# A two-layer decoder trunk on one core: the first loads in the order of use, on two queues, with the start of the schedule rearranged

## The chip, the core and the metric

The kernel runs on one core of a Trainium2 chip. A core has five engines that take instructions in order and wait for each other by semaphores: TensorE (PE) multiplies and transposes, ScalarE (ACT) and VectorE (DVE) work elementwise, GpSimd (POOL) sets up constants and issues some transfers, SyncE (SP) issues most transfers. Transfers between memory and the core's buffers are carried out by 16 DMA engines. The metric is the device time of one execution in microseconds (us), as the median of several; lower is better. The kernel before takes 962.69 us (three runs, 961.73 to 963.36).

## The reference, cut to what matters

Layer 0 is a forgetting attention, layer 1 a dilated window attention. Each is followed by an embedding term; 512 tokens, model width 1024, everything in float32.

```python
h = x
# layer 0
h = h + fox_mixer(rms_norm(h, fox_norm[0]), fox_w_in[0], fox_b_f[0], fox_w_out[0])
h = h + (p[0] @ ple_w_up[0]) * sigmoid(h @ ple_w_gate[0])
# layer 1
h = h + dilated_mixer(rms_norm(h, dil_norm[0]), dil_w_in[0], dil_w_out[0])
h = h + (p[1] @ ple_w_up[1]) * sigmoid(h @ ple_w_gate[1])
return rms_norm(h, final_norm)

# fox_mixer begins with
proj = rms_norm(h) @ w_in          # q, k, v, z (1024 columns each) and f (16 columns)
c = cumsum(log_sigmoid(f + b_f))   # the forget gates
# logit[t, s] = q_t . k_s / 8 + c[t] - c[s], causal softmax, values, silu(z), @ w_out
```

The work at the start needs x, p[0], the norm's gain, ple_w_up[0] and fox_w_in.

## The kernel before, in words

**Products in three parts.** A float32 operand is kept as two parts: `hi`, its copy rounded to the type that PE multiplies in one go (ACT, line 86 for weights and 436 for activations), and `lo`, the rest (DVE, lines 87 and 437). A product is hi·hi + hi·lo + lo·hi, so three matmuls (lines 298, 299, 300).

**Weights** come through the class `Stream` as granules in a fixed list: first two halves of `ple_w_up[0]` (256 rows by 512 columns each), then four granules of `fox_w_in` for the first half of v (I call them F0 to F3, 512 KB each), the 16 columns of f, four more granules for v, and so on. There are four buffers for raw granules and five for split ones. `prefetch(n)` issues the loads up to granule n on SP's queue; a granule's buffer is free for its next load when both parts of the split are made.

**The start**, which the change touches, has these steps.
1. POOL makes the identity matrix `ident` (lines 443, 444).
2. SP issues the loads. p[0] comes in two halves of its 256 columns (`load_p0`, line 527), each followed by one half of granule 0 (line 71); then block 0 of x (line 536), granule 1 (line 73), block 1, the gain (line 465), blocks 2 and 3, F0 to F2.
3. `p_columns` transposes p (PE, line 507), two groups of four, and splits it to `pT`; after each group one half of granule 0 is split (`then(k)`, line 509).
4. `up_rows` computes p @ ple_w_up (48 matmuls, in two column halves of four token blocks). ACT evacuates each block (line 517) to a tile `upo`, of which there are three, and SP stores it to a scratch tensor `up_dram` at once (line 518). It is read back only at the end of layer 0.
5. `start_block(b)` normalises a block of 128 tokens: two square sums on ACT (line 487), nine small DVE instructions for 1/sqrt (`rstd_of`, lines 476 to 481), the product `xn` on DVE (line 552). `side` then pushes eight transposes (PE, line 456) and the split into `xnT`. Blocks 0 and 1 are started inside `up_rows`, blocks 2 and 3 inside step 6.
6. `token_rows` computes the first half of v (I call it V0): 96 matmuls, 24 per token block, over F0 to F3.
7. Then `f_rows`: 16 matmuls for the forget gates, whose first is line 625. `f_evac` computes the gates on ACT and DVE; POOL sends the result `cc` to where the scores read it.

The order in which instructions stand on each engine is made by a scheduler from the dependencies and the order in which the code issues them. `tc.issue_after(i)` keeps what stands under it behind instruction `i` in that order. Layer 0's heads, the middle part and layer 1 follow; the change doesn't touch their code.

## Time and profile before

| What | Value |
|---|---|
| Median of three runs | 962.69 us |
| The profiled execution's own time | 960.73 us |
| Its span, first to last instruction | 958.9 us |
| PE busy | 935.7 us, 98% of the span |
| DVE busy | 702.0 us, 73% |
| ACT busy | 503.3 us, 52% |
| Identity matrix finished by POOL | 1.37 us |
| PE's products start 0.43 us apart until, 0.23 from | 12.54 us |
| Last stores of line 518 in layer 0 issued | 27.21 us |
| cc sent by POOL (line 646) | 66.40 us |
| First score product on PE (line 682) | 89.25 us |

The profile is of one execution. Times in the rows further down are counted from its first instruction. A busy share is an average over stages: what the start costs is read from the first 50 us, in which each engine's instructions can be followed one by one. The time between two starts on PE is the pace of its products; the duration of one is longer, since they overlap.

### The profile page before, as it was taken

The numbers are of one execution on the slowest core, as the hardware profiler recorded it, in microseconds if no ns is written. First come the engines' busy times: TensorE is split into PE (matmuls) and PEld (weight loads), VectorE is DVE, ScalarE is ACT, GpSimd is POOL, SyncE is SP. The second block draws the span as 40 slices with busy tenths as digits, with TensorE's granted clock in tenths as the row PEclk, the third lists the DMA queues.
The fourth block names the chain that finished last, engine by engine and source line by source line (L and its number), as shares of the span: only waits on it lengthen the run. The fifth ranks groups of instructions, "written<-read, shape, count | busy, mean of one in ns | idle before, by whom it ended". The sixth has DMA issues, their size and how long they took to land.

```text
span 958.9 us, 15802 instructions
## 1 busy us (share of the span) xinstructions
PE 935.7 (98%) x6000; PEld 841.2 (88%) x6000; DVE 702.0 (73%) x1421; ACT 503.3 (52%) x926; POOL 56.7 (6%) x119
## 2 busy tenths in 40 slices
PE   6999999999999999999999999999999999999996
PEld 5888888888888887899999999999999999987885
DVE  5765877777764478887897887758788797675446
ACT  7455766766752248543565554443446455564233
POOL 0000000000027000100000000010000000010000
PEclk9999999999999999999999999999999999999999
DMA  8453222221146227353323223335332322256102
GB/s 295 146 154 88 67 67 67 67 66 67 67 154 217 90 88 241 113 152 88 111 70 108 69 66 111 111 107 135 96 103 74 104 79 68 99 163 232 68 0 89
DMA packets 126588, 104.58 MB, mean 109 GB/s; under 512 B 14736, under 2 KB 105872, under 8 KB 126512
## 3 DMA queue, kind: packets, MB, share of 16 engines
q1 hardware_dynamic: 121728, 90.59, 31.0%
q0 software_dynamic: 4608, 12.72, 4.1%
q8 instruction: 47, 0.77, 0.3%
q14 instruction: 29, 0.24, 0.1%
q10 hardware_dynamic: 176, 0.26, 0.1%
HBM read 92.93 MB, written 10.55 MB: 108 GB/s over the span
## 4 chain that ended last, share of the span: by engine, by line
PE 82%; DVE 7%; DMA 5%; ACT 4%; issue 2%; SPq 1%; DVEq 0%; POOLq 0%; ACTq 0%
PE ps L347 8%; PE ps L349 8%; PE ps L348 8%; PE ps L300 8%; PE ps L298 8%; PE ps L299 8%; PE ps L328 4%; PE ps L330 4%; PE ps L329 4%; PE ps L404 3%; PE ps L406 3%; PE ps L407 3%; PE ps L715 2%; PE ps L1024 2%; DMA oth<-stb 2%
## 5 line engine op out<-in xcount | busy, mean ns | idle before, releaser
L87 DVE TENSOR_TENSOR wlo<-wraw,whi 128x1024 fp32r<-128x1024 f32 (+1 forms) x78 | 94.4, 1211 | 102.8 <-ACT whi L86 102.2
L347 PE MATMUL ps<-comb,whi 128*128 128x256 f32 x448 | 131.0, 292 | 0.0
L86 ACT ACTIVATE whi<-wraw 128x1024 fp32r<-128x1024 f32 (+1 forms) x78 | 81.7, 1048 | 92.7 <-PE ps L300 60.2
L349 PE MATMUL ps<-comb,wlo 128*128 128x256 f32 x448 | 127.0, 284 | 0.0
L348 PE MATMUL ps<-comb,whi 128*128 128x256 f32 x448 | 126.7, 283 | 0.0
L347 PE MATMUL ps<-xn2T,whi 128*128 128x256 f32 x336 | 97.1, 289 | 0.0
L108 ACT ACTIVATE whi<-ws 128x1024 fp32r<-128x1024 f32 x56 | 59.2, 1057 | 68.7 <-PE ps L348 64.9
L349 PE MATMUL ps<-xn2T,wlo 128*128 128x256 f32 x336 | 95.1, 283 | 0.0
L348 PE MATMUL ps<-xn2T,whi 128*128 128x256 f32 x336 | 95.0, 283 | 0.0
L348 PEld LDWEIGHTS ps<-comb,whi 128*128 128x128 f32 x448 | 85.8, 192 | 0.4
L347 PEld LDWEIGHTS ps<-comb,whi 128*128 128x128 f32 x448 | 85.8, 192 | 0.4
L349 PEld LDWEIGHTS ps<-comb,wlo 128*128 128x128 f32 x448 | 85.8, 192 | 0.0
L109 DVE TENSOR_TENSOR wlo<-ws,whi 128x1024 fp32r<-128x1024 f32 x56 | 68.3, 1219 | 14.7 <-ACT whi L108 14.7
L328 PE MATMUL ps<-xnT,whi 128*128 128x512 f32 x192 | 78.5, 409 | 0.0
L330 PE MATMUL ps<-xnT,wlo 128*128 128x512 f32 x192 | 75.4, 393 | 0.0
L329 PE MATMUL ps<-xnT,whi 128*128 128x512 f32 x192 | 75.0, 391 | 0.0
L108 ACT ACTIVATE whi<-wraw 128x1024 fp32r<-128x1024 f32 (+1 forms) x56 | 47.3, 844 | 36.7 <-PE ps L348 20.9
L348 PEld LDWEIGHTS ps<-xn2T,whi 128*128 128x128 f32 x336 | 64.4, 192 | 0.0
L347 PEld LDWEIGHTS ps<-xn2T,whi 128*128 128x128 f32 x336 | 64.4, 192 | 0.0
L349 PEld LDWEIGHTS ps<-xn2T,wlo 128*128 128x128 f32 x336 | 64.3, 191 | 0.0
L109 DVE TENSOR_TENSOR wlo<-wraw,whi 128x1024 fp32r<-128x1024 f32 (+1 forms) x56 | 53.0, 950 | 2.1 <-ACT whi L108 2.0
L298 PE MATMUL ps<-whi,hT 128*128 128x512 f32 (+1 forms) x136 | 51.7, 380 | 0.0
(245 smaller groups left out, 2466.1 us busy)
## 6 DMA issues: line engine op xcount, KB each, us to landing
wraw<-in_dil_w_in_dram SPq DMA_DIRECT2D x80, 512.0 KB, 3.8
wraw<-in_fox_w_in_dram SPq DMA_DIRECT2D x32, 512.0 KB, 4.2
wraw<-in_ple_w_gate_dram SPq DMA_DIRECT2D x16, 512.0 KB, 3.7
up_dram<-upo SPq DMA_DIRECT2D x16, 256.0 KB, 4.1
wraw<-in_fox_w_out_dram SPq DMA_DIRECT2D x8, 512.0 KB, 3.4
up<-up_dram POOLq DMA_DIRECT2D x8, 512.0 KB, 5.7
wraw<-in_dil_w_out_dram SPq DMA_DIRECT2D x8, 512.0 KB, 3.4
x_in<-in_x_dram SPq DMA_DIRECT2D x4, 512.0 KB, 9.0
```

The lines of the kernel that those rows point to most:

```text
L86: ACT.activation(hi[:, k], t[:, k], AF.Copy)
L87: DVE.tensor_tensor(lo[:, k], t[:, k], f32(hi)[:, k], OP.subtract)
L108: ACT.activation(hi[:, :n], src, AF.Copy)
L109: DVE.tensor_tensor(lo[:, :n], src, f32(hi[:, :n]), OP.subtract)
L298: PE.matmul(o, xh, wh[:, kk, c0:c1], start=first, stop=False)
L299: PE.matmul(o, xh, wl[:, kk, c0:c1], start=False, stop=False)
L328: PE.matmul(t, wh[:, k, :], xh, start=(k == 0), stop=False)
L329: PE.matmul(t, wh[:, k, :], xl, start=False, stop=False)
L330: PE.matmul(t, wl[:, k, :], xh, start=False, stop=(k == KT - 1))
L347: PE.matmul(o, ah, bh, start=(first and k == 0), stop=False, skip_group_check=not first)
L348: PE.matmul(o, ah, bl, start=False, stop=False, skip_group_check=not first)
L349: PE.matmul(o, al, bh, start=False, stop=(last and k == 3), skip_group_check=not first)
```

## The change

Six edits, all in the start, and one in the gate evaluation.

1. p[0] is one load (`load_p`, line 501 of the new file: 4 KB that lie together per partition) on SP's queue. The first half of granule 0 goes out on ACT's queue at the same time, the second on SP's. After them come block 0 of x, granule 1, the gain, F0, block 1, F1, block 2, F2, block 3, F3.
2. Fourteen transposes of `ident` into an unused bank stand ahead on PE (line 540), with no reader.
3. Granule 0's first half is split after p's first transposes are issued and before pT's first split; the second half's split is kept behind that of pT on ACT.
4. One table load, of the set that has both logarithm and exponential, stands at the start. The load of the other set, which the scheduler had put at the very start, is kept behind `cc`; the two loads inside `f_evac` fall away.
5. Blocks 0 and 1 of x are started at steps 3 and 7 of `up_rows`, blocks 2 and 3 at steps 3 and 6 of V0 (before: 4 and 7, 1 and 4); `side.flush()` after `up_rows` falls away; `xn` has one buffer, not two.
6. The eight stores of `up_rows` are kept in a list and issued in V0's steps 8 to 15, behind the load of F3; `upo` has eight buffers, not three.

The core of the diff:

```diff
             if i == 0:
                 for k in range(nk):
-                    self.before[k]()
-                    SP.dma_start(t[:, k, :], src[:, k, :])
+                    (ACT, SP)[k].dma_start(t[:, k, :], src[:, k, :])
             else:
-                SP.dma_start(t[:, :, :cw], src)
+                load = SP.dma_start(t[:, :, :cw], src)
+                if i == g_v[0][3]:
+                    last["load"] = load
...
+            if k == 0:
+                then(0)
             split_out(pT[0][:, k, :], pT[1][:, k, :], t)
-            then(k)
+            if k == 0:
+                with tc.issue_after(last["act"].ins):
+                    then(1)
...
-                u = pool.tile([P, 512], F32, tag="upo", bufs=3, name=nm("upo"))
+                u = pool.tile([P, 512], F32, tag="upo", bufs=(8, 3)[L], name=nm("upo"))
                 ACT.activation(u, t, AF.Copy, scale=0.5)
-                SP.dma_start(up_dram[L][b][:, c * 512:(c + 1) * 512], u)
+                store = lambda c=c: SP.dma_start(up_dram[L][b][:, c * 512:(c + 1) * 512], u)
+                if L == 0:
+                    stores.append(store)
+                else:
+                    store()
...
-        pin = sp.tile([P, NB, 256], F32, tag="pin", bufs=1, name=nm("pin"))
-
-        def load_p0(k):
-            SP.dma_start(pin[:, :, k * P:(k + 1) * P],
-                         p[0, 0, :, k * P:(k + 1) * P].rearrange("(p b) c -> p b c", p=P))
-
-        ws.before = [lambda: load_p0(0), lambda: load_p0(1)]
+        pin = load_p(0, sp)
         ws.prefetch(1)
+        ACT.preload_act_table_set("natural_log_exp_and_others")
+        idle = bank(7)
+        for n in range(14):
+            PE.transpose(idle[:, n % 4 * P:(n % 4 + 1) * P], ident, ident)
...
         load_x(0)
         ws.prefetch(2)
+        gain = load_gain(fox_norm, sp, "gain")
+        ws.prefetch(3)
         load_x(1)
-        gain = load_gain(fox_norm, sp, "gain")
+        ws.prefetch(5)
         load_x(2)
         load_x(3)
-        ACT.preload_act_table_set("natural_log_exp_and_others")
...
-            xn = sp.tile([P, D], F32, tag="xn", bufs=2, name=nm("xn"))
+            xn = sp.tile([P, D], F32, tag="xn", bufs=1, name=nm("xn"))
...
                 side.tick()
-                if n in (4, 7):
-                    start_block((n - 4) // 3)
-            side.flush()
+                if n in (3, 7):
+                    start_block((n - 3) // 4)
         for n, _ in enumerate(token_rows(xnT, g_v[0], blk, v_evac(0), group=4)):
             side.tick()
-            if n in (1, 4):
-                start_block(2 + (n - 1) // 3)
+            if n in (3, 6):
+                start_block(1 + n // 3)
+            if n > 7:
+                with tc.issue_after(last["load"].ins):
+                    stores.pop(0)()
...
-        ACT.activation(cc[:16], u, AF.Copy)
+        done = ACT.activation(cc[:16], u, AF.Copy)
         DVE.tensor_tensor(cc[64:80], u, f32(cc[:16]), OP.subtract)
-        ACT.preload_act_table_set("exp_and_others")
+        with tc.issue_after(done.ins):
+            ACT.preload_act_table_set("exp_and_others")
```

How the order of instructions moves, at three places. The new file's lines are two or more higher than the old one's for the same code.

SP's queue, its first loads, before (`pin` is p, `wraw` a raw granule, of w_up or w_in, `x_in` a block of x):

```order
L527 DMA pin_88<-in_p_dram 128x4x128
L71 DMA wraw_89<-in_ple_w_up_dram 128x512
L527 DMA pin_88<-in_p_dram 128x4x128
L71 DMA wraw_89<-in_ple_w_up_dram 128x512
L536 DMA x_in<-in_x_dram 128x1024
L73 DMA wraw_96<-in_ple_w_up_dram 128x2x512
L536 DMA x_in<-in_x_dram 128x1024
L465 DMA gain_99<-in_fox_norm_dram 128x1024
L536 DMA x_in<-in_x_dram 128x1024 x2
L73 DMA wraw_132<-in_fox_w_in_dram 128x2x512
```

The same of the changed kernel; the other half of granule 0 stands on ACT:

```order
L501 DMA pin_88<-in_p_dram 128x1024
L70 DMA wraw_90<-in_ple_w_up_dram 128x512
L545 DMA x_in<-in_x_dram 128x1024
L72 DMA wraw_111<-in_ple_w_up_dram 128x2x512
L467 DMA gain_113<-in_fox_norm_dram 128x1024
L72 DMA wraw_115<-in_fox_w_in_dram 128x2x512
L545 DMA x_in<-in_x_dram 128x1024
L72 DMA wraw_118<-in_fox_w_in_dram 128x2x512
L545 DMA x_in<-in_x_dram 128x1024
L72 DMA wraw_120<-in_fox_w_in_dram 128x2x512
```

F0 (`wraw_132`, now `wraw_115`) moves from the eleventh load to the seventh, counting ACT's, and ahead of blocks 1 to 3 of x.

DVE, from the sixth small step of block 0's 1/sqrt to its `xn` and the first step of block 1, before:

```order
L480 SCALAR_TENSOR_TENSOR rstd_198<-rstd_198 128x1
L481 SCALAR_TENSOR_TENSOR rstd_198<-rstd_198 128x1
L480 SCALAR_TENSOR_TENSOR rstd_198<-rstd_198 128x1
L481 SCALAR_TENSOR_TENSOR rstd_198<-rstd_198 128x1
L552 SCALAR_TENSOR_TENSOR xn_208<-x_in,rstd_198,gain_99 128x1024
L476 TENSOR_SCALAR rstd_259<-ss_254 128x1
```

The same of the changed kernel:

```order
L482 SCALAR_TENSOR_TENSOR rstd_192<-rstd_192 128x1
L88 TENSOR_TENSOR wlo_206<-wraw_115,whi_205 128x1024
L483 SCALAR_TENSOR_TENSOR rstd_192<-rstd_192 128x1
L482 SCALAR_TENSOR_TENSOR rstd_192<-rstd_192 128x1
L483 SCALAR_TENSOR_TENSOR rstd_192<-rstd_192 128x1
L562 SCALAR_TENSOR_TENSOR xn_202<-x_in,rstd_192,gain_113 128x1024
L478 TENSOR_SCALAR rstd_265<-ss_260 128x1
```

The low part of F0's split now stands behind the sixth of the nine steps; before, it stood behind `xn` of block 1.

ACT, from the split of granule 1 on, before (`junk` is a square sum of a block of x, `upo` an evacuation of p @ w_up):

```order
L86 ACTIVATE whi_128<-wraw_96 128x1024
L487 ACTIVATE junk_194,ss_193<-x_in 128x512
L517 ACTIVATE upo_144<-ps_127 128x512
L487 ACTIVATE junk_196,ss_193<-x_in 128x512
L487 ACTIVATE junk_255,ss_254<-x_in 128x512
L517 ACTIVATE upo_154<-ps_147 128x512
```

The same of the changed kernel:

```order
L87 ACTIVATE whi_148<-wraw_111 128x1024
L489 ACTIVATE junk_188,ss_187<-x_in 128x512
L523 ACTIVATE upo_158<-ps_147 128x512
L523 ACTIVATE upo_167<-ps_160 128x512
L489 ACTIVATE junk_190,ss_187<-x_in 128x512
L87 ACTIVATE whi_205<-wraw_115 128x1024
```

Two evacuations stand between the two square sums of block 0, and the high part of F0's split follows them, ahead of block 1's square sums. On PE (not shown) 14 transposes of `ident` stand first, the first two token blocks of `up_rows` take turns, and before V0 there are eight transposes of block 0 alone, where there were those of blocks 0 and 1; block 1's stand inside V0's first token block, behind 21 matmuls.

## Rows read from the trace of the kernel before

**Rows 1.** Timeline, PE, start: start us, us, engine, line, operation, out<-in, [idle before]

```profile
4.04 1.09 PE L507 MATMUL ps<-ident,pin 128*128 128x128 f32 x4 [4.04 <-DMA pin<-in_p_dram]
6.47 1.11 PE L507 MATMUL ps<-ident,pin 128*128 128x128 f32 x4 [1.34 <-DMA pin<-in_p_dram]
9.39 0.80 PE L298 MATMUL ps<-whi,pT 128*128 128x512 f32 x1 [1.80 <-ACT pT L436]
...
11.69 0.63 PE L300 MATMUL ps<-whi,pT 128*128 128x512 f32 x1
12.12 0.62 PE L298 MATMUL ps<-whi,pT 128*128 128x512 f32 x1
```

**Rows 2.** Timeline, PE, transposes of block 0, V0's first product, the gates' first

```profile
19.22 1.03 PE L456 MATMUL ps<-ident,xn 128*128 128x128 f32 x8
20.01 0.48 PE L298 MATMUL ps<-whi,pT 128*128 128x512 f32 x1
...
24.77 0.48 PE L298 MATMUL ps<-whi,xnT 128*128 128x512 f32 x1
...
48.81 0.39 PE L625 MATMUL ps<-xnT,whi 128*128 128x512 f32 x1
```

**Rows 3.** Windows: from:to, us, busy of each engine, granted clock, DMA share, GB/s

```profile
4.00:6.00 2.00, 1.09 (x4) 0.71 (x4) 0.00 (x0) 0.61 (x1) 0.00 (x0) 1.00 0.80 203
...
8.00:10.00 2.00, 0.61 (x2) 0.50 (x2) 1.12 (x2) 1.60 (x3) 0.00 (x0) 1.00 1.01 392
```

**Rows 4.** DMA issues in windows around single ones: KB, us from issue to landing

```profile
pin<-in_p_dram SPq DMA_DIRECT2D x1, 256.0 KB, 3.1
wraw<-in_ple_w_up_dram SPq DMA_DIRECT2D x1, 256.0 KB, 3.8
x_in<-in_x_dram SPq DMA_DIRECT2D x1, 512.0 KB, 6.6
gain<-in_fox_norm_dram SPq DMA_DIRECT2D x1, 512.0 KB, 9.3
```

**Rows 5.** Timeline, SP, the issues of these four transfers

```profile
0.81 0.66 SPq L527 DMA_DIRECT2D pin<-in_p_dram  x1
1.52 0.60 SPq L71 DMA_DIRECT2D wraw<-in_ple_w_up_dram  x1
...
3.43 0.43 SPq L536 DMA_DIRECT2D x_in<-in_x_dram  x1
...
4.99 0.74 SPq L465 DMA_DIRECT2D gain<-in_fox_norm_dram  x1
```

**Rows 6.** Timeline, ACT, granule 1's split and block 0's square sums

```profile
11.39 1.06 ACT L86 ACTIVATE whi<-wraw 128x1024 fp32r<-128x1024 f32 x1 [1.56 <-DMA wraw<-in_ple_w_up_dram]
12.35 0.61 ACT L487 ACTIVATE junk<-x_in 128x512 f32<-128x512 f32 x1
...
12.96 0.58 ACT L517 ACTIVATE upo<-ps 128x512 f32<-128x512 f32 x1
13.44 0.62 ACT L487 ACTIVATE junk<-x_in 128x512 f32<-128x512 f32 x1
```

**Rows 7.** Timeline, DVE: a split, the first small step, xn, two parts of xnT

```profile
12.47 1.23 DVE L87 TENSOR_TENSOR wlo<-wraw,whi 128x1024 fp32r<-128x1024 f32 x1 [1.71 <-ACT whi L86]
14.18 0.21 DVE L476 TENSOR_SCALAR rstd<-ss 128x1 f32<-128x1 f32 x1 [0.48 <-ACT junk L487]
...
16.02 1.28 DVE L552 SCALAR_TENSOR_TENSOR xn<-x_in,rstd,gain 128x1024 f32<-128x1024 f32 x1
...
21.48 1.28 DVE L437 TENSOR_TENSOR xnT<-ps,xnT 128x512 fp32r<-128x512 f32 x2
```

**Rows 8.** Timeline, PE, late in layer 1, after its longest pause there

```profile
864.29 0.30 PE L1024 MATMUL ps<-ident,p 128*128 128x128 f32 x1 [2.69 <-DVE p L1008]
...
866.72 0.40 PE L300 MATMUL ps<-whi,ozT 128*128 128x512 f32 x1
866.95 0.40 PE L298 MATMUL ps<-whi,ozT 128*128 128x512 f32 x1
```

More of the change, by code (lines that the diff above doesn't have):

```diff
@@ L174, in get @@
             return self.parts.pop(i)
+    last = {}
     ws = Stream()
@@ L431, in quad_rows @@
         yield
-    last = {}
     def split_out(hi, lo, src):
@@ L515, in evac @@
             def evac(b, t):
-                u = pool.tile([P, 512], F32, tag="upo", bufs=3, name=nm("upo"))
+                u = pool.tile([P, 512], F32, tag="upo", bufs=(8, 3)[L], name=nm("upo"))
                 ACT.activation(u, t, AF.Copy, scale=0.5)
-                SP.dma_start(up_dram[L][b][:, c * 512:(c + 1) * 512], u)
+                store = lambda c=c: SP.dma_start(up_dram[L][b][:, c * 512:(c + 1) * 512], u)
[3 more added lines that the diff above has]
+                    store()
             yield from token_rows(pT, [granules[c]], blk, evac, nk=2)
+    stores = []
     with tc.tile_pool(name="start", bufs=1) as sp:
         consts()
-        pin = sp.tile([P, NB, 256], F32, tag="pin", bufs=1, name=nm("pin"))
-        def load_p0(k):
-            SP.dma_start(pin[:, :, k * P:(k + 1) * P],
-                         p[0, 0, :, k * P:(k + 1) * P].rearrange("(p b) c -> p b c", p=P))
-        ws.before = [lambda: load_p0(0), lambda: load_p0(1)]
+        pin = load_p(0, sp)
         ws.prefetch(1)
+        ACT.preload_act_table_set("natural_log_exp_and_others")
+        idle = bank(7)
+        for n in range(14):
+            PE.transpose(idle[:, n % 4 * P:(n % 4 + 1) * P], ident, ident)
         x_in = base.tile([P, NB, D], F32, tag="qkh", bufs=1, name="x_in")
```

## The prediction

> **What bounds the kernel now.** I read the whole-span shares first, then the waits and the timeline of TensorE (PE) at the start, then the DMA queue, then ScalarE (ACT) and VectorE (DVE) in the same microseconds. The shares (in the table on time and profile) say that PE is busy 98% of the span: from about 25 us on it runs without a break that matters, and a change to the first stage can only move the point at which that unbroken run begins. So the whole question is how early PE gets there. I take as the mark the first product of the forget gates (line 625), which starts at 48.81 us [rows 2]; all that follows it stands in the same order in both kernels apart from a few neighbouring pairs on DVE.
>
> Up to that mark PE has 144 products of 512 columns and 40 transposes to do. At the full pace products start 0.23 us apart [rows 8], so 144 cost 32.7 us, and the transposes about 5. The other 11 us are lost in three ways. PE waits 4.04 us for the first half of p, 1.34 us for the second and 1.80 us for pT [rows 1]. The products from 9.39 to 12.5 us (in the table) start 0.43 us apart instead of 0.23 [rows 1]: the pace of 1.2 GHz instead of 2.4, although the granted clock in the windows there reads 1.00 [rows 3]; PE had done only two groups of four transposes with lulls between before it. And V0, the first product group on xnT, can only start at 24.77 [rows 2], because the normalised rows xn come late out of the chain load, square, rstd, xn on ACT and DVE [rows 6, 7].
>
> **The loads.** Before, p came as two transfers of 512-byte pieces, and all the queue's first 8 us were slow: 203 GB/s in 4 to 6 us against 392 GB/s from 8 us [rows 3]. p's first quarter MB was issued at 0.81 and took 3.1 us (landed 3.9), the first quarter of w_up 1.52 + 3.8 = 5.3, x block 0 3.43 + 6.6 = 10.0, the gain 4.99 + 9.3 = 14.3 [rows 4, 5]. Between the last two stand three half MB, so one takes 1.43 us. Now p is one transfer with 4 KB per partition. Its end lies between 3.9 (where the first quarter landed) and 5.3 (where the second transfer did); at the 392 GB/s of the later row the second quarter takes 0.67 us, and I take 4.6. From there, at 1.43 each: w_up's first half 6.0, x block 0 7.5, w_up's second half 8.9, gain 10.3, the first piece of w_in (call it F0) 11.7. The other end is that the places in the queue land when they landed before: 8.2, 10.0, 11.4, 12.9 and 14.3.
>
> The trace shows one busy hardware queue there, SP's; a transfer issued by ACT beside it isn't in these rows. What the second queue certainly saves is SP's issue, 0.60 us for the w_up row [rows 5]; I put that at nothing, because packets and not issues are late. The Trainium skill's page "DMA: Bandwidth & Descriptors", section "Issuing engines are not separate DMA queues", speaks against more: transfers issued from ACT and SP run on the same 16 engines and interleave, so only sequencer time is saved. By it p shares the engines with w_up's first quarter and lands up to 0.67 us later, 5.3, which is the upper end above; the sum would not move, since it hangs on F0.
>
> **The first products.** The 14 transposes of the identity wait only for POOL, which is done at 1.4 (in the table), and run at the pace of a group of four (1.09 us, so at most 0.27 each) [rows 1]: to 5.2 us at the latest. p's first transposes are then held up by 0 to 0.6 us and end between 5.6 and 6.2; ACT has w_up's first part and pT some 0.9 us later, so PE's first product starts near 6.5 to 7 instead of 9.39. On paper that is 2.5 us or more, and with the full pace 1.5 more. But neither is the end of the chain: by 24 + 12 products PE is at the transposes of xn block 0 at about 14.7 (or 15.7 at the slow pace), and these are late.
>
> **xn block 0**, the term that decides. w_up's second half lands at 8.9. ACT then does in its order the split (0.96 to the next start), one square sum (0.61), now two evacuations (0.48 each) instead of one, and the other square sum (0.74 to DVE's first step): 12.2 [rows 6, 7]. DVE needs nine small steps, 1.84 us from 14.18 to 16.02, and xn, 1.28 [rows 7]. In the new order the low split of F0 stands behind the sixth step: 1.2 us of steps (13.4), then the split, whose high part ACT has made by 13.2: 1.2 us (14.6), the last three steps 0.6, xn 1.28: 16.5, against 17.30 before. So PE waits some 1.8 us there, which is new.
>
> **V0.** Eight transposes take 0.79 us to the next product's start and twelve products 2.7 [rows 2]: V0 starts at 16.5 + 3.5 = 20.0 instead of 24.77, mostly because only one block's transposes stand ahead of it and not two. From V0 to the mark it took 24.04 us. It now holds a third group of eight transposes (0.8), and a wait for xn of block 1: DVE has before it four splits (4.9), two xnT parts (1.3), nine steps (1.84) and xn (1.28) [rows 7], which serially end at 25.8, while PE wants it 21 products after 20.0, at 24.8. The wait is between 0 (steps hidden between the others) and 1.0; I take 0.5. The mark: 20.0 + 24.04 + 0.8 + 0.5 = 45.3, so 3.5 us earlier.
>
> **The rest, at nothing.** Two table loads leave the gate chain and one moves behind cc. cc is sent by POOL at 66.40, and PE reads what it feeds only at 89.25 (both in the table); the 20 us between hide it either way. The held stores: behind them on SP stand loads of w_in that V1 wants about 4 us after the mark, and on DVE the memset of `wide`, which reuses their buffers; the last store was issued at 27.2 us before (in the table), and now each goes out behind a load that is issued by then, so either has over 10 us. The preload behind cc costs ACT 1.3 us in a stage in which ACT idles. xn with one buffer makes block 3's xn wait for block 2's transposes, some 1 us before anyone wants it.
>
> Sum: the profiled execution took 960.73 us (span 958.9), so 957.2; it was 1.96 us under the median of the runs, 962.69. Against that median: 962.69 - 3.5 = 959.2.
>
> **Rivals.**
> The queue is no faster (landings at the other end). w_up's second half 11.4, F0 14.3: the square sums end at 14.6, the six steps at 15.8, F0's split at 17.0, xn at 19.0, V0 at 22.5 and the mark at 47.7 or so: 1.1 us gained, 961.6. For it: rows 4 show nothing faster this early. Against it: the 203 GB/s stand exactly where the 512-byte pieces are [rows 3].
>
> The lull drops PE to the low pace. PE pauses some 1.8 us ahead of xn block 0. If it then ran as from 9.39 to 12.54 [rows 1] (and the table), 3.15 us would do 1.6 us of work: 1.9 us gained, 960.8. Against it: late in the kernel PE stood idle 2.69 us, and 2.5 us on its products start 0.23 us apart [rows 8]. The Trainium skill's page "TensorE: Matmul & The Clock Gate", section "HAM oscillation", states that waits for transfers between bursts put the array back to the low clock; by that rule this rival's time holds. The trace disagrees for a pause of that length.
>
> Slower: F0's split in the middle of the rstd chain. DVE takes its instructions in order, so until F0 has landed no xn is made. From landing to the mark are 0.96 + 1.2 + 0.6 + 1.28 + 3.5 + 25.3 = 32.8 us, so from a landing at 16.0 on the kernel is slower, us for us; at 18, 2 us slower, 964.7. That is 4.3 us after my estimate and 1.7 after the worst row at that place.
>
> The idle transposes do nothing (the pace stays low to 9 us): PE is at xn block 0 at 15.7, still ahead of 16.5. Same time as the forecast, and counted in it.
>
> **Chances.** Forecast, 2.3 to 4.8 us gained: 0.68. Queue no faster, 0.3 to 2.3: 0.17. Lull, about 1.9: 0.06. More than 4.8 (landings earlier than I take, no wait for xn block 1): 0.05. Slower, by F0 or by something I don't see: 0.04. A measurement of this kernel tells 0.2% (1.9 us) from no change; so the border is 960.8. Faster: the forecast, the large gain, half of the lull, a little of the second, 0.78; within 0.2%: 0.18; slower: 0.04. The range runs from 5.4 us gained (957.3) to 0.9 (961.8), which leaves out some 0.15.
>
> **What would show it.** First product at 6 to 7 us; starts 0.23 us apart by 9; a pause of PE ahead of xn block 0 that DVE ends; F0's split inside the rstd steps without waiting on a load; V0 at 19 to 21.5; the mark at 44 to 46.5; after it the same distances as before. It is wrong if F0 or w_up's second half lands over 2 us later than above, if PE doesn't pause at xn block 0 at all, or if the gain at the mark is not in the total.

## The result, and the profile after

Timed beside each other, the kernel before took 963.36 us (median of 5 runs, 961.73 to 967.98) and the changed one 958.25 (955.82 to 959.16): a ratio of 0.9937, 95% interval 0.9907 to 0.9966, or 6.1 us less (3.3 to 9.0). Two further comparisons of the same two kernels, with more runs, gave 0.9956 (0.9940 to 0.9972) and 0.9958 (0.9944 to 0.9971): 4.2 and 4.0 us. The forecast was 3.5, its range 0.9 to 5.4: the first comparison's 6.1 lies above it, the two later ones in it. The profiled execution of the changed kernel took 959.16 us (span 957.4, before 958.9), the longest of its five; between the two profiled executions lie only 1.6 us. What made these numbers differ is the subject of what follows.

The start first. Timeline of PE in the changed kernel: start, duration, engine, line, operation, the wait before it and what ended it.

```profile
1.43 3.25 PE L540 MATMUL ps<-ident 128*128 128x128 f32 x14 [1.43 <-POOL ident L446]
5.43 1.10 PE L509 MATMUL ps<-ident,pin 128*128 128x128 f32 x8 [0.76 <-DMA pin<-in_p_dram]
6.78 0.50 PE L300 MATMUL ps<-whi,pT 128*128 128x512 f32 x1 [0.25 <-ACT pT L438]
...
7.59 0.39 PE L301 MATMUL ps<-wlo,pT 128*128 128x512 f32 x1
7.82 0.39 PE L302 MATMUL ps<-whi,pT 128*128 128x512 f32 x1
...
16.57 1.06 PE L458 MATMUL ps<-ident,xn 128*128 128x128 f32 x8 [1.34 <-DVE rstd L478]
...
20.23 0.39 PE L300 MATMUL ps<-whi,xnT 128*128 128x512 f32 x1
...
24.99 1.03 PE L458 MATMUL ps<-ident,xn 128*128 128x128 f32 x8
...
44.96 0.39 PE L638 MATMUL ps<-xnT,whi 128*128 128x512 f32 x1
```

Against [rows 1, 2]: the first product is at 6.78 instead of 9.39, and from 7.1 products start 0.23 us apart; one new wait of 1.34 us, ahead of xn block 0, that DVE ends; V0 at 20.23 instead of 24.77; the mark at 44.96 instead of 48.81. The transposes of xn block 1 (24.99) wait for nothing.

The loads, DMA issues of the first 4 us: KB, us from issue to landing.

```profile
pin<-in_p_dram SPq DMA_DIRECT2D x1, 512.0 KB, 4.6
x_in<-in_x_dram SPq DMA_DIRECT2D x1, 512.0 KB, 5.9
wraw<-in_ple_w_up_dram SPq DMA_DIRECT2D x1, 512.0 KB, 6.8
gain<-in_fox_norm_dram SPq DMA_DIRECT2D x1, 512.0 KB, 7.6
wraw<-in_ple_w_up_dram ACTq DMA_DIRECT2D x1, 256.0 KB, 4.8
...
wraw<-in_fox_w_in_dram SPq DMA_DIRECT2D x1, 512.0 KB, 8.6
```

With the issues on SP at 0.81, 1.72, 2.19, 2.67 and 3.18 these are landings at 5.4 (p), 7.6 (x block 0), 9.0 (w_up's second half), 10.3 (gain) and 11.8 (F0). Windows of the changed kernel (columns as in [rows 3]), the two that answer to [rows 3] and three late ones:

```profile
4.00:6.00 2.00, 1.24 (x9) 0.84 (x8) 0.00 (x0) 0.40 (x1) 0.00 (x0) 1.00 1.00 352
8.00:10.00 2.00, 2.00 (x10) 1.61 (x10) 0.76 (x2) 1.00 (x2) 0.00 (x0) 1.00 1.03 380
860.00:862.00 2.00, 0.44 (x2) 0.47 (x3) 1.93 (x7) 0.81 (x2) 0.00 (x0) 0.85 0.98 367
862.00:864.00 2.00, 2.00 (x8) 1.53 (x7) 0.20 (x1) 2.00 (x5) 0.00 (x0) 0.50 0.85 303
864.00:866.00 2.00, 2.00 (x11) 1.63 (x10) 0.79 (x2) 0.33 (x1) 0.00 (x0) 0.80 0.14 54
```

From 4 to 6 us the DMA engines move 352 GB/s where they moved 203. The last three windows are new: behind the pause of [rows 8] the granted clock falls to 0.50, that is 1.2 GHz instead of 2.4. PE's timeline there:

```profile
861.56 0.45 PE L1037 MATMUL ps<-ident,p 128*128 128x128 f32 x1 [2.82 <-DVE p L1021]
...
863.08 0.63 PE L300 MATMUL ps<-whi,ozT 128*128 128x512 f32 x1
863.51 0.63 PE L301 MATMUL ps<-wlo,ozT 128*128 128x512 f32 x1
```

Products start 0.43 us apart where they started 0.23 apart before. From the first of these transposes to the end of the span it is 95.9 us, in the trace before 94.6: the low clock cost this execution 1.2 us. Another 1.0 went between the mark and 845 us, in exchanges through memory (the offsets in the table below), and 0.1 in the pause itself. So 3.85 us gained at the mark were 1.5 at the end. An exchange is this: in each head of the second layer SP stores small tiles of numbers (`own`) to memory in eight transfers, to `sta` and `stb`, POOL reads them back in another order (`oth`), and DVE makes weights from both (`alpha`), for which PE's transposes of p wait.

### The profile page after: what moved, and what is told of

Read it like the earlier page. It is cut to its first block, busy times and chain, and to the rows that moved or that the text cites. A ratio compares the mean times of both kernels' runs of the same rounds, so it can differ in the third digit from the quotient of the medians.

```text
span 957.4 us, 15824 instructions
## 1 busy us (share of the span) xinstructions
PE 938.1 (98%) x6014; PEld 843.6 (88%) x6014; DVE 700.8 (73%) x1421; ACT 501.3 (52%) x924; POOL 56.9 (6%) x119
## 4 chain that ended last, share of the span: by engine, by line
PE 82%; DVE 7%; DMA 5%; ACT 4%; issue 2%; SPq 1%; DVEq 0%; ACTq 0%; POOLq 0%
PE ps L349 8%; PE ps L350 8%; PE ps L351 8%; PE ps L302 8%; PE ps L300 8%; PE ps L301 8%; PE ps L330 4%; PE ps L332 4%; PE ps L331 4%; PE ps L406 3%; PE ps L408 3%; PE ps L409 3%; PE ps L728 2%; DMA stb<-own 2%; PE ps L1037 1%
## 5 line engine op out<-in xcount | busy, mean ns | idle before, releaser
L88 DVE TENSOR_TENSOR wlo<-wraw,whi 128x1024 fp32r<-128x1024 f32 (+1 forms) x78 | 94.6, 1212 | 100.0 <-ACT whi L87 99.7
```

The source lines that it names most:

```text
L88: DVE.tensor_tensor(lo[:, k], t[:, k], f32(hi)[:, k], OP.subtract)
```

## The experiments

Each comparison behind the first has its own runs of the kernel before beside it (medians 960.9 to 962.1). The offset at 845 us is worked out from the starts of PE's products: how much later than in the run late_idle (below) the same product stands, counted from the mark, just ahead of the last head. It tells what an execution lost between the mark and there, in waits for the exchanges and at the low clock behind such waits.

| kernel | median us | ratio to before, 95% | mark in the trace | offset at 845 us |
|---|---|---|---|---|
| before, first trace | 963.36 | | 48.81 | 0.5 |
| again_before | 961.37 | 0.9994 (0.9975-1.0013) | 47.88 | 1.6 |
| changed, first trace | 958.25 | 0.9937 (0.9907-0.9966) | 44.96 | 1.5 |
| again_after | 957.96 | 0.9956 (0.9940-0.9972) | 44.92 | -0.3 |
| after_3 | 957.89 | 0.9958 (0.9944-0.9971) | 44.99 | 0.4 |
| late_idle | 956.52 | 0.9943 (0.9922-0.9964) | 44.95 | 0 |
| late_idle_before | 961.06 | 0.9999 (0.9985-1.0013) | 48.83 | 1.3 |
| no_idle | 958.52 | 0.9962 (0.9949-0.9976) | 48.43 | -1.1 |
| one_queue | 957.39 | 0.9960 (0.9947-0.9973) | 47.35 | -0.9 |
| stores_inline | 961.05 | 0.9989 (0.9977-1.0001) | 48.57 | -0.7 |
| f0_behind | 960.14 | 0.9992 (0.9979-1.0005) | 49.45 | 0.1 |
| p_one | 959.13 | 0.9965 (0.9950-0.9979) | 47.54 | -0.1 |
| p_rows | 959.12 | 0.9976 (0.9966-0.9987) | 45.94 | -1.5 |
| p_halves (two traces) | 962.35 | 1.0018 (1.0003-1.0032) | 47.37, 46.70 | 5.9, 2.9 |
| p1_halves | 961.93 | 1.0003 (0.9988-1.0018) | 45.04 | 4.1 |
| alpha3 (two traces) | 953.67, 953.30 | 0.9911 (0.9891-0.9931) | 45.08, 45.15 | 0.0, -0.5 |
| alpha3_before | 958.51 | 0.9959 (0.9945-0.9974) | 47.88 | 2.0 |
| p_halves_alpha3 | 959.23 | 0.9974 (0.9962-0.9986) | 47.19 | 4.0 |

**Both kernels again.**

> The kernel before, once more as it stands. Theory A: the change earns 3.85 us at the mark (first product of the forget gates: 48.81 before, 44.96 after) and nothing behind it; what the two profiles differ in behind the mark (910.1 us from the mark to the end of the span before, 912.4 after) is the last head of the second layer, whose exchange through memory and whose pause of PE come out differently from execution to execution. It expects here the mark at 48.5 to 49.1, and from the mark to the end anything from 909.5 to 914, the difference to 910.1 being found between 840 and 870 us. Rival B: the change does something to the late part too; then before repeats itself: 910.1 within 0.5 us, products 0.23 us apart behind the late pause, no lower clock there.

> The changed kernel, once more as it stands. Theory A: mark at 44.7 to 45.3; from the mark to the end 909.5 to 914 as for the kernel before; median 956.5 to 959. Rival B (the change slows the late part in the profile, or speeds it in the timed runs): 912.4 within 0.5 again with the lower clock behind the pause at about 861 us, or, if it speeds the late part, under 909 from the mark to the end.

> The changed kernel a third time, for the size of the gain on another comparison: 3.0 to 4.5 us under before (theory A), mark 44.8 to 45.1; rival 5.5 to 6.5 us under before.

The change's mark repeats to 0.1 us (44.92 to 44.99); that of before does not (47.88 and 48.81: its second half of p lets PE wait 0.60 us or 1.34). From the mark to the end stand 910.0 us in again_before, as in the first trace, but 911.1 in again_after, again with the clock at 0.50 behind a pause, of 3.22 us. The traces alone thus favoured rival B's slow late part, while the timed runs gave 4.2 us.

**The late pause filled.** Ahead of the last head's transposes of p:

```
+        if j == 7:
+            warm = bank(7)
+            for n in range(14):
+                PE.transpose(warm[:, n % 4 * P:(n % 4 + 1) * P], ident, ident)
```

> The changed kernel with 14 transposes of the identity into a free bank put in front of the last head's transposes of p, where PE stood idle 2.82 us and then ran eight products and more 0.43 us apart (granted clock 0.50 at 862 to 864 us). Theory A: they take 14 x 0.14 = 1.9 us of the pause, the clock stays 1.00 between 858 and 868 us, the products behind the pause start 0.23 us apart, and an execution in which the clock would have dropped gains 1.5 us; as I don't know how often it drops, the median is 0 to 1.5 us under that of the changed kernel, 0.8 as the middle. Rival: the pause is not what lowers the clock there (before had one of 2.69 us without a loss), so the low stretch comes as often with the 14 as without, and the time is the same within 0.3 us, or 0.3 longer if they hold up the transposes of p.

> The kernel before with the 14 identity transposes in front of the last head's transposes of p (late_idle's edit without the change). Theory A now: the pause there lowers the clock in most executions of either kernel; before's two profiles (1.00 throughout) are two of the minority, which its timed runs show by mean clocks: 10 of 37 at 0.998 or so without it, the others lower and slower. So the median falls by 0.8 to 1.6 us under that of before beside it, about what late_idle gained on the changed kernel (1.4 us), and the mean clock reads 0.997 or 0.998 in every run. Rival: the change itself set the low clock off (its PE reaches the pause earlier, with more behind it), before has it seldom: no gain within 0.4 us, and the change then earned 1.4 us more at the start than it kept.

Timeline of PE in late_idle:

```profile
856.88 1.69 PE L1034 MATMUL ps<-ident 128*128 128x128 f32 x14
860.11 0.61 PE L1041 MATMUL ps<-ident,p 128*128 128x128 f32 x3 [1.54 <-DVE p L1021]
...
860.80 0.39 PE L301 MATMUL ps<-wlo,ozT 128*128 128x512 f32 x1
861.03 0.39 PE L302 MATMUL ps<-whi,ozT 128*128 128x512 f32 x1
```

The pause is down to 1.54 us, the pace stays at 0.23, and from the mark to the end it is 909.85 us, 1.3 to 2.6 less than in the three plain traces of the changed kernel. The mean granted clock of an execution was 0.997 or 0.998 in all six runs, but in only 2 of the 18 timed executions of the plain changed kernel (the rest 0.995 or 0.996). The median fell by 1.4 us, though the two ratios' intervals overlap. On the kernel before the same edit gave nothing (0.9999), though ten of its twelve executions read 0.997 or more: the rival held there. Before reads 0.997 or more in 62 of the 131 executions timed beside these runs, so without the edit too it runs at the low clock less often than the changed kernel. Its late pause was 2.69 and 1.50 us without a loss; the changed kernel's was 2.82, 3.22 and 3.10, with a loss each time. And 14 transposes are no insurance: in late_idle_before 1.91 us were left, and the clock fell all the same.

**The identity transposes taken away.** With them gone the scheduler puts ACT's split of F0 ahead of two evacuations, so the test is not clean.

```
-        idle = bank(7)
-        for n in range(14):
-            PE.transpose(idle[:, n % 4 * P:(n % 4 + 1) * P], ident, ident)
```

> The changed kernel without its 14 identity transposes at the start. The rival in the prediction (they earn nothing): products 0.43 us apart up to about 10 us, PE at the xn block 0 transposes 1.0 to 1.3 us later than the 15.23 of the changed kernel, still ahead of xn at 16.5, so the mark at 44.96 within 0.3. The other theory: the slow products also hold up ACT's evacuations and with them the square sums behind them, and PE reaches xn block 0 after 16.6: mark at 45.5 to 46.5, and the time 0.5 to 1.5 us longer.

The first products ran 0.43 us apart from 6.95 to 9.2. xn block 0 came 2.3 us later than in the changed kernel, PE waited 2.11 us for it and then lost its clock (0.50 at 20 to 22 us): mark 48.43. That trace was one of the longer of its runs; the median lies 0.6 us over again_after, inside both intervals. The mark is later than either theory had it. What the 14 earn is not settled.

**The second queue and the form of p's transfer.**

First one_queue, then p_halves:

```
-                    (ACT, SP)[k].dma_start(t[:, k, :], src[:, k, :])
+                    SP.dma_start(t[:, k, :], src[:, k, :])
```

```
-        pin = load_p(0, sp)
+        for k in range(2):
+            SP.dma_start(pin[:, :, k * P:(k + 1) * P],
+                         p[0, 0, :, k * P:(k + 1) * P].rearrange("(p b) c -> p b c", p=P))
```

> The changed kernel with the first quarter of w_up issued by SP, between p and the second quarter, instead of by ACT; PE, DVE and ACT keep their orders. As the prediction has it (packets are late, not issues; the second queue earns nothing): the mark within 0.3 of 44.95. Rival 1: SP's issues behind it come 0.42 us later and so does everything: mark 45.4. Rival 2: the ACT queue's quarter took bandwidth from p: without it p lands sooner (4.6 to 5.0 instead of 5.1 to 5.4), the first product comes 0.2 to 0.5 us earlier, and the mark does not move, since xn block 0 is the end of the chain.

> The changed kernel with p in two transfers of 512-byte pieces on SP, as before; no other instruction is moved. Forecast's theory (the pieces slow the queue): first transposes of p wait for both halves one after the other, w_up's second half and x block 0 land 1 to 2.4 us later than in the changed kernel (ACT's split of granule 1 at 10.0 to 11.4 instead of 9.0), xn block 0 as much later, the mark 0.8 to 2.4 us later (45.8 to 47.4). Rival (the queue was slow for being cold, or for the order, not for the pieces): split of granule 1 within 0.4 of 9.0 and the mark at 44.9 to 45.3.

In one_queue p landed 3.4 us after its issue, in the changed kernel 4.6, beside ACT's quarter of w_up (4.2 to 4.6 in all ten traces that have both):

```profile
pin<-in_p_dram SPq DMA_DIRECT2D x1, 512.0 KB, 3.4
```

The time is that of the changed kernel, so in total the second queue earns nothing. The mark says otherwise, against the expectation: in this trace it is 47.35, and the 2.4 us were made up behind it: beside the mean of the three plain traces 1.5 by 845 us and 1.7 at the last head, where the clock held behind a pause of 2.86 us. One trace doesn't tell whether that is so in every execution. w_up's second half came 0.8 us later, xn block 0 with it, and here the lull rival took place, at xn block 0 itself:

```profile
17.40 1.94 PE L458 MATMUL ps<-ident,xn 128*128 128x128 f32 x8 [2.26 <-DVE rstd L478]
...
19.57 0.63 PE L301 MATMUL ps<-wlo,pT 128*128 128x512 f32 x1
19.99 0.63 PE L302 MATMUL ps<-whi,pT 128*128 128x512 f32 x1
```

p_halves has ACT's split of granule 1 at 11.40 instead of 9.00 and its mark 1.7 to 2.4 us later, as the forecast's theory wants. Yet it is 4.4 us slower than again_after (1.0018 of the time of before), and 915.7 us lie behind its mark. The next runs follow this.

**p in one transfer alone, in the kernel before; p in two transfers of long pieces; the held stores.** First p_one, then p_rows, then stores_inline:

```
-            SP.dma_start(pin[:, :, k * P:(k + 1) * P],
-                         p[0, 0, :, k * P:(k + 1) * P].rearrange("(p b) c -> p b c", p=P))
+        pin = load_p(0, sp)
+        ws.before = [lambda: None, lambda: None]
```

```
-        SP.dma_start(pin, p[L, 0].rearrange("(p b) c -> p b c", p=P))
+        for h in range(2 - L):
+            q = slice(64 * h, 64 * h + 64) if L == 0 else slice(0, P)
+            SP.dma_start(pin[q], p[L, 0].rearrange("(p b) c -> p b c", p=P)[q])
```

```
-                u = pool.tile([P, 512], F32, tag="upo", bufs=(8, 3)[L], name=nm("upo"))
+                u = pool.tile([P, 512], F32, tag="upo", bufs=3, name=nm("upo"))
...
-                if L == 0:
-                    stores.append(store)
-                else:
-                    store()
+                store()
```

> The kernel before with one edit of the change alone: p in one transfer with 4 KB per partition at its first place in SP's queue, the rest of the orders as before. p_halves (the changed kernel with the two halves back) had its mark 2.4 us later and ran 5 us slower. Theory (the 512-byte pieces hold up all that stands behind them in the queue): here the landings behind p come 1 to 2.4 us sooner, the mark falls from 47.9-48.8 to 45.5-47.5, and the time by 1.5 to 3 us against before. Rival (the order and the warm PE are what counts; p_halves was slow because its second quarter of w_up came late and PE, waiting 1.78 us for it, lost its clock): mark within 0.5 of 47.9 to 48.8, time within 0.7 us of before.

> The changed kernel with the first p in two transfers of 64 partitions each, 4 KB per partition: two transfers, as p_halves, but the long pieces of the change (some of SP's issues of stores and loads behind 11 us change places). If the 512-byte pieces make p_halves slow (mark 46.7 to 47.4), the mark stays at 44.8 to 45.6 here, the offset by 725 us within -0.9 to 0.8 and the median within 0.7 us of the changed kernel. If the second transfer by itself does (one more issue of 0.4 us, one more place in the queue): mark 45.4 to 47.4, and 1 to 4 us over the changed kernel.

> The changed kernel with its first stores as before: three buffers, each store issued where its evacuation stands (some neighbouring rows of DVE and PE around 17 to 30 us fall into another order with it). Forecast (the held stores are worth nothing): mark within 0.4 of 44.95 and the time within 0.7 us of the changed kernel (957.4 to 958.7 where before is 961 to 962). Rival: ACT's evacuations wait for a free buffer while the stores stand in the queue behind the loads of x and w_in, the square sums of the next blocks behind them, and xn of block 1 comes late: mark 46 to 48.

> p_halves once more, for a second trace: its first had the mark at 47.37 and 915.7 us from there to the end, where nine other traces have 908.7 to 913.4. If the late part is by chance (exchange transfers and the clock behind the pauses they make), it is 909 to 913 here; if the two halves of p slow the late part by themselves, 914 to 917 again. Mark 47.0 to 49.

p_one by itself earns 3.4 us (2.0 to 4.8), more than its mark shows (0.3 to 1.3). p_rows: the second transfer by itself moves p's first transposes to 6.03, PE loses its clock behind that wait of 1.49 us, and the mark is 45.94, 1.0 late; a part of p_halves' loss at the mark (1.7 to 2.4) can thus be the second transfer and not the pieces. Behind the mark p_rows loses nothing (offset -1.5). p_halves_2 is slow behind its mark again (914.3): not chance. And the held stores, which I had costed at nothing, are worth 3.6 us at the mark (with them a few neighbouring rows of PE, DVE and ACT moved). ACT in stores_inline, then PE:

```profile
19.21 0.60 ACT L523 ACTIVATE upo<-ps 128x512 f32<-128x512 f32 x1 [3.11 <-DMA up_dram<-upo]
```

```profile
28.42 1.07 PE L458 MATMUL ps<-ident,xn 128*128 128x128 f32 x8 [1.15 <-DVE rstd L478]
```

With three buffers the fourth evacuation waits for the first store, which stands in the queue behind the loads now put ahead; behind it on ACT are the next splits.

**F0's split behind xn block 0.**

```
+            if i == g_v[0][0]:
+                with tc.issue_after(last["xn"].ins):
+                    DVE.tensor_tensor(lo[:, k], t[:, k], f32(hi)[:, k], OP.subtract)
```

> The changed kernel with the low split of F0 pinned behind xn of block 0 on DVE instead of inside its rstd steps (some later rows of PE and DVE fall into another order with it). If the forecast's chain is all (xn block 0 ends it): xn block 0 at 13.9 to 15.2 instead of 15.14 to 16.42, no wait of PE ahead of its transposes, V0 and the mark up to 1.2 us earlier (43.7 to 44.2). Rival: DVE has no idle time between 12.3 and 24.8 us, so the split is only paid later; xn of block 1 stays at 23.5 to 24.8 and PE, earlier now, waits there for 0.8 to 1.2 us: mark at 44.6 to 45.1, same time.

xn block 0 came at 14.16, as planned, but neighbouring rows fell into another order, and on DVE xn of block 1 now stands behind a split that waits 2.95 us for ACT:

```profile
28.18 1.06 PE L462 MATMUL ps<-ident,xn 128*128 128x128 f32 x8 [2.88 <-DVE rstd L482]
```

Mark 49.45 and 2.2 us over again_after. Where the change put the split is better than the place that shortens the chain to xn block 0.

**The exchanges of the second layer.** p1_halves moves no instruction of PE, DVE, ACT or POOL: only the second layer's p, loaded from 284.5 us on under other work, comes in two transfers of 512-byte pieces.

```
-        SP.dma_start(pin, p[L, 0].rearrange("(p b) c -> p b c", p=P))
+        for k in range(1 + L):
+            c = slice(k * P, (k + 1) * P) if L else slice(0, 256)
+            SP.dma_start(pin[:, :, c], p[L, 0, :, c].rearrange("(p b) c -> p b c", p=P))
```

> The changed kernel with the second layer's p (loaded behind 300 us, under other work) in two transfers of 512-byte pieces instead of one; the first p as the change has it, PE, DVE, ACT and POOL in the same order. Between the mark and 725 us the seven traces with the first p in halves lie 0.7 to 2.3 us behind late_idle's (mean 1.6), the twelve with it in one transfer -0.9 to 1.2 (mean -0.1). Theory C: what shifts the exchanges of the heads at 545 to 745 us is the count of packets that SP's queue has carried by then (121,728 with the halves, 120,672 without), wherever they stand: mark 45.0, 1.0 to 2.3 us behind by 725 us, median 1 to 2 us over the changed kernel (958.9 to 960 where before is 962). Theory D: only the start counts, or the shift is chance: within 0.7 us of the changed kernel, -0.9 to 0.8 by 725 us.

Same mark (45.04), 4 us slower than after_3. The fifth head's exchange, row by row, first POOL in the changed kernel:

```profile
722.80 0.56 POOL L999 DMA_DIRECT2D oth<-stb  x1 [3.85 <-DMA stb<-own]
```

and in p1_halves POOL, DVE and PE:

```profile
723.97 0.56 POOL L1001 DMA_DIRECT2D oth<-stb  x1 [5.96 <-DMA stb<-own]
```

```profile
729.22 0.17 DVE L1012 TENSOR_TENSOR alpha<-own,oth 128x8 f32<-128x8 f32 x1 [1.96 <-DMA oth<-stb]
```

```profile
735.86 0.33 PE L1039 MATMUL ps<-ident,p 128*128 128x128 f32 x1 [1.82 <-DVE p L1023]
...
737.52 0.41 PE L350 MATMUL ps<-comb,whi 128*128 128x256 f32 x1
737.73 0.41 PE L351 MATMUL ps<-comb,wlo 128*128 128x256 f32 x1
```

DMA issues from 718 to 725 us (KB, median us from issue to landing), in the changed kernel, then in p1_halves:

```profile
stb<-own SPq DMA_DIRECT2D x4, 1.0 KB, 1.5
oth<-stb POOLq DMA_DIRECT2D x1, 4.0 KB, 3.6
```

```profile
stb<-own SPq DMA_DIRECT2D x4, 1.0 KB, 2.0
oth<-stb POOLq DMA_DIRECT2D x1, 4.0 KB, 5.2
```

The four small stores of stb are issued 4.96 us after sta's in both. Here they take longer, the last of them 3.26 us instead of 1.50, and the load behind them 5.2 instead of 3.6; alpha waits, PE pauses 1.82 us and loses its clock (0.21 us between starts of 256 columns instead of 0.12). Every trace with 512-byte pieces of p in SP's queue has an offset at 845 us of 0.5 to 5.9 (8 traces, mean 2.8), every other one of -1.5 to 1.5 (12 traces, mean -0.3). So what the exchanges take hangs on the form of transfers long gone. p_halves and p1_halves show it, which keep the computing engines' order of the changed kernel and run 4 us slower (p_halves in part by its mark), while p_rows, with one more transfer for the first p but long pieces, has no such offset. By what path is open: theory C's count of packets does not hold as put, since before carried the more packets too and lies at 0.5 to 2.0, while the kernels with the new order and pieces lie at 2.9 to 5.9, and p1_halves had only 0.5 of its offset by 725 us.

**A version that beats both.** In the changed kernel DVE waits 2.73 us for the last head's exchange with three splits queued behind the waiting instruction:

```profile
855.59 0.17 DVE L1010 TENSOR_TENSOR alpha<-own,oth 128x8 f32<-128x8 f32 x1 [2.73 <-DMA oth<-stb]
855.69 1.23 DVE L88 TENSOR_TENSOR wlo<-wraw,whi 128x1024 fp32r<-128x1024 f32 x1
...
857.59 1.22 DVE L88 TENSOR_TENSOR wlo<-wraw,whi 128x1024 fp32r<-128x1024 f32 x1
...
859.56 1.22 DVE L88 TENSOR_TENSOR wlo<-wraw,whi 128x1024 fp32r<-128x1024 f32 x1
...
861.13 1.07 DVE L1021 TENSOR_SCALAR p<-p,alpha 128x128 f32<-128x128 f32 x4
```

```
-            DVE.tensor_tensor(lo[:, k], t[:, k], f32(hi)[:, k], OP.subtract)
+            last["wlo"] = DVE.tensor_tensor(lo[:, k], t[:, k], f32(hi)[:, k], OP.subtract)
...
-        DVE.tensor_tensor(w[:, 2, :], own[:, :, 0], oth[:, :, 0], OP.min)
+        if j == 7:
+            while ws.ns < ws.nu + 3:
+                ws.prefetch(ws.ns + 1)
+                ws._split(ws.ns)
+                ws.ns += 1
+        with tc.issue_after(last["wlo"].ins) if j == 7 else ExitStack():
+            DVE.tensor_tensor(w[:, 2, :], own[:, :, 0], oth[:, :, 0], OP.min)
```

> A version meant to beat both: the changed kernel, with two of DVE's three low splits (1.14 us each) that stand between the last head's first alpha step and its transposes of p put ahead of that step, into the 2.7 us in which DVE waits for the exchange transfer. If the pause of PE there (2.8 to 3.2 us) is made by these splits, p is ready 2.3 to 2.9 us earlier, the pause shrinks below 1 us, the clock stays 1.00 behind it, and the time falls by 2.3 us and by up to 1.5 more in executions that lost the clock: median 954 to 955.5 where the changed kernel has 958. Rival: the exchange ends later than the splits and the gain is spent on the next step (the products behind want splits that come later, or the end waits for something else): within 0.7 us of the changed kernel.

> alpha3 once more, beside alpha3_before: median 953 to 954.5, mark 44.9 to 45.2, 905.5 to 908 from the mark to the end, no pause of PE over 1 us and no lower clock between 840 and 870 us.

> The kernel before with alpha3's edit at the last head (two low splits ahead of the wait for the exchange). It takes the late pause out of the kernel before as alpha3 took it out of the changed one, so that the two compare without it. Theory A (the change earns what the mark shows, 3.0 to 3.9 us, and the rest of the 6.1 us first measured was chance of the late part): 3.0 to 4.2 us above alpha3_2 beside it (956.7 to 957.9 if that is 953.7 again), mark 47.9 to 48.8 and 905.5 to 908 from the mark to the end. Rival (the change earns some 2 us more somewhere that the mark does not show): 5.5 to 6.5 us above alpha3_2, 959.2 to 960.2.

> p_halves with alpha3's edit. Its mark was 2.4 and 1.8 us later than the changed kernel's, its time 4.4 to 5. If the surplus of 2.5 us lies in the last head's pause: 2.0 to 2.6 us above alpha3_2 (955.5 to 956.5). If it lies in an earlier exchange (its two traces had PE waiting 1.87 and 1.96 us at 738 to 740 us, and 2.19 at 588 in one, where the others show none over 0.85): 4 to 5 us above alpha3_2, with a pause of 1.5 us or more ahead of the transposes of p near 738 us again, and a lower clock behind it in some executions.

DVE in alpha3:

```profile
851.39 1.21 DVE L88 TENSOR_TENSOR wlo<-wraw,whi 128x1024 fp32r<-128x1024 f32 x1
...
853.13 1.22 DVE L88 TENSOR_TENSOR wlo<-wraw,whi 128x1024 fp32r<-128x1024 f32 x1
854.26 0.16 DVE L1016 TENSOR_TENSOR alpha<-own,oth 128x8 f32<-128x8 f32 x1
...
857.15 1.07 DVE L1027 TENSOR_SCALAR p<-p,alpha 128x128 f32<-128x128 f32 x4
```

Two splits run where DVE waited, alpha no longer waits, PE's long pause is gone and with it the low clock: 953.67 us, and 953.30 when repeated (0.9911, 0.9894 to 0.9927), 8.5 us under before and 4.3 to 4.6 under the changed kernel. With this edit in both kernels they differ by 5.2 us (ratios 0.9959 and 0.9911: 4.6), between theory A's 3.0 to 4.2 and the rival's 5.5 to 6.5: part of the gain does lie behind the mark. p_halves_alpha3 stayed 5.9 us over alpha3_2, more than either branch foresaw; it waits 2.17 us at 588 and 1.44 at 739. Beside alpha3_2's trace 2.0 us of its surplus stand at the mark and 4.5 between the mark and 845 us, none in the last pause.

## Why the prediction was right and where it was wrong

**Right: the start, step by step.** w_up's second half 9.0 (put at 8.9), x block 0 7.6 (7.5), gain 10.3 (10.3), F0 11.8 (11.7), first small step of DVE 12.29 (12.2), F0's low split 13.37 inside the steps (13.4), xn block 0 done 16.4 (16.5), PE's wait there 1.34 (1.8), V0 20.23 (20.0), mark 44.96 (45.3). p landed at 5.4, not 4.6. The sentence from the Trainium skill's page "DMA: Bandwidth & Descriptors", section "Issuing engines are not separate DMA queues", gave 5.3. The traces agree: p took 4.2 to 4.6 us beside ACT's transfer and 3.4 and 3.6 where w_up's quarter stands behind it on SP's queue (one_queue, p_one). p's later landing moved nothing, as forecast. Missized was the wait for xn block 1 (0.5 put, none measured).

**Wrong: "after it the same distances as before".** This is the step that failed: the sum took the gain at the mark for the gain of the kernel and put all that follows at nothing. At the mark the gain is 3.3 us (mean of four traces with before's start, 48.35, against six with the changed start, 45.01). By 845 us another 1.2 has come to it: the mean offset there is 1.4 in those four and 0.2 in those six. p_one, p_halves and p1_halves show where it comes from, as far as it goes: with p in one transfer the exchanges of several heads of the second layer are shorter; by what path is open. 3.3 and 1.2 make 4.5, and with alpha3 in both kernels, which takes the last head's pause out, 4.6 to 5.2 were timed.

The last head gives part back, in the plain kernels only. From the same product at 845 us to the end the three traces of the changed kernel take 110.8 to 111.3 us, the two of before 108.3 and 109.5: the pause is longer and the clock fell behind it, at 1.2 to 1.4 us. But before's two traces are not its rule, as the mean clocks show: 0.997 or more in 62 of its 131 executions, in 2 of 18 of the changed kernel. At like clock the two kernels' medians lie 4.2 us apart below 0.997 (962.4 and 958.2) and 4.7 above (960.5 and 955.8, the latter of two executions). So the timed gain of 4.0 to 4.2 is some 4.5 less what the changed kernel loses by its clock falling more often; why its last exchange ends later is not shown.

The first comparison's 6.1 is partly chance: it has five executions of each, one of before at 967.98, and its interval reaches from 3.3 to 9.0. The forecast of 3.5 lies inside all three intervals, which is partly luck too, since it left out a gain and a loss behind the mark. The forecast time 959.2 lies above the changed kernel's medians, 957.9 to 958.3.

**Wrong: the reference.** I took the profiled execution of before as 1.96 us under its median and carried the same distance over. For the changed kernel's first trace it was 0.9 over. Executions of one kernel differ by the exchanges and the clock.

**Wrong: the argument against the lull.** One pause of 2.69 us without a loss [rows 8] was no evidence. Over all 20 traces, of 25 pauses of 1.8 to 3.4 us behind the first product, the clock fell behind 18; of those between 1.2 and 1.6 there behind none, but ahead of the first product p_rows lost it behind 1.49. The Trainium skill's page "TensorE: Matmul & The Clock Gate", section "HAM oscillation", on which that rival leaned, tells of longer waits than the 1.8 us forecast here, so the rival stretched it, and one pause of 2.69 us could not contradict it. In these traces the clock fell behind most of the shorter waits as well, not behind all. At xn block 0 the changed kernel's pause is short (1.2 to 1.6) and cost the clock in none of its traces; in one_queue and no_idle, with 2.26 and 2.11, it did.

**Wrong: the held stores "at nothing".** In the new order of loads holding them avoids a wait of 3.1 us on ACT, and without it the change earned about 1 us (0.9989, an interval that takes in no gain). I had named what stands behind the stores, not what waits for their buffers.

## What to carry to other kernels

Read not only what a moved load delays next, but which small transfers on a critical exchange come later; here one hidden load's form was worth 4 us, lost in exchanges hundreds of us behind it. Where an in-order engine waits for a transfer, put ready work ahead of the waiting instruction: that edit was worth as much as the whole change. Take a kernel's late stage from several traces before adding its distances to a gain: one execution shows one draw of the exchanges and of the clock.

## What the runs showed of the hardware that I had not expected

- The granted clock fell to 0.50 behind 18 of 25 pauses of 1.8 to 3.4 us, for some 3 us each (once 6.8); at the last head that cost 1.2 to 1.6 us. Pauses of nearly the same length at the same place went either way (2.86 us kept in one_queue, 2.85 lost in p_rows).
- Small stores of 1 KB landed later (POOL's wait for them 5.96 us against 3.85, the last store 3.26 us after its issue against 1.50) with another form of a load that had ended hundreds of us before, with the same order on every computing engine.
- p, 512 KB in 4-KB pieces, landed 3.4 us after its issue with no transfer from another queue beside it and 4.2 to 4.6 beside 256 KB from ACT's queue.
